# A Strassen form for the FFN input product of a float32 decoder trunk

## The chip, the cores and the metric

The kernel runs on one core of one Trainium2 chip. The metric is the time of one execution on the device in microseconds (us). The core's engines are TensorE (PE in the profile; its weight loads are listed apart as PEld), VectorE (DVE), ScalarE (ACT), GpSimd (POOL) and SyncE (SP), which here only issues loads. Matrix products are written to PSUM, eight banks of 128 x 512 float32; everything else lies in SBUF.

## The reference

A decoder trunk of two layers on 512 tokens of 1024 features. Each layer is: h += 0.5 * FFN(norm(h)), a token mixer (retention in layer 0, forgetting attention in layer 1), h += 0.5 * FFN(norm(h)) with other weights, and a gated input per layer. A last norm follows. The FFN, which runs four times:

```python
def swiglu(x, w_in, w_out):          # w_in 1024 x 5632, w_out 2816 x 1024
    g, u = jnp.split(x @ w_in, 2, axis=-1)
    return (jax.nn.silu(g) * u) @ w_out

def rmsnorm(x, w):
    y = xf * lax.rsqrt(jnp.mean(xf * xf, axis=-1, keepdims=True) + EPS)
    return y * w
```

## The kernel before

Activations lie with features on the partitions: `h` is eight tiles of 128 features x 512 tokens. A float32 operand is kept as two float32r parts, a rounded high one and the remainder as the low one. A product is three matmuls, high x high, high x low and low x high (`mm3`, lines 199 to 202); a high part is a copy on ScalarE and a low part a subtraction, usually on VectorE.

Weights come as chunks of 128 x 1024 in the order of use (`W.plan`). `take` returns the next one and emits the load, copy and subtraction of the chunks up to LOOKAHEAD = 3 further on (lines 79 to 83 and 42 to 55). SP's queue does the loads into three raw tiles; the split parts have four pairs of tiles. In the mixers and in the gated stages the subtraction goes to POOL (`W.low`). The last KEPT chunks stay in SBUF for the final stage, which handles the tokens in two parts of 256.

`Norm.block(b)` makes the operand of the next product from a finished block of h: the gain goes into the split (`halves`), and the squares are summed by ScalarE and POOL (`square`). The token's scale is put on after the product (`rows`).

One FFN (`ffn`, lines 292 to 330) goes over 22 blocks of 128 features. For each the gate and the up chunk are multiplied (`proj`, 8 blocks of input features x 3 matmuls each, 512 columns), then `finish` makes silu(g r) * u and splits it. The output product runs over the 8 blocks of h, each with 22 inner blocks x 3 matmuls in one PSUM bank, evacuated once (lines 326 to 330). The kernel's first two chunks are loaded in narrow parts (`emit_parts`), so that the first products follow x as it comes.

The order of instructions on TensorE is that of the program; on the other engines a planner orders them by program order and its own estimate of what is ready. A tile is written again only after its last reader.

Of the kernel before, what the change touches and what calls it, by code (L numbers as in the profile page):

```python
# [27 lines left out]
LOOKAHEAD = 3  # L28
KEPT = 6


class Weights:
    """Streams weight chunks [128, <=1024] in the order in which they are used, each split
    exactly into two float32r parts, high and low."""

    def __init__(self, nc, raw_pool, split_pool):
        self.nc, self.raw_pool, self.split_pool = nc, raw_pool, split_pool
        self.plan, self.ready, self.used = [], [], 0
        self.low = nc.vector
        self.limit = None  # L40

    def emit(self, upto):
        nc = self.nc
        while len(self.ready) < min(upto, self.limit):
            src = self.plan[len(self.ready)]
            n = src.shape[1]
            raw = self.raw_pool.tile([P, 1024], F32, name="wraw")
            hi = self.split_pool.tile([P, 1024], F32R, name="whi")
            lo = self.split_pool.tile([P, 1024], F32R, name="wlo")
            nc.sync.dma_start(out=raw[:, :n], in_=src)  # L50
            nc.scalar.copy(hi[:, :n], raw[:, :n])  # L51
            self.low.tensor_tensor(  # L52
                out=lo[:, :n], in0=raw[:, :n], in1=hi[:, :n].bitcast(F32), op=ALU.subtract
            )
            self.ready.append((hi, lo))

    def emit_parts(self, count, parts):
        """The first chunks, in narrow parts and side by side."""
        nc = self.nc
        tiles = [  # L60
            (
                self.raw_pool.tile([P, 1024], F32, name="wraw"),
                self.split_pool.tile([P, 1024], F32R, name="whi"),
                self.split_pool.tile([P, 1024], F32R, name="wlo"),
            )
            for _ in range(count)
        ]
        for k0, k1 in parts:
            cs = slice(k0 * P, k1 * P)
            for src, (raw, hi, lo) in zip(self.plan, tiles):  # L70
                nc.sync.dma_start(out=raw[:, cs], in_=src[:, cs])
                nc.vector.tensor_copy(hi[:, cs], raw[:, cs])
                nc.vector.tensor_tensor(  # L73
                    out=lo[:, cs], in0=raw[:, cs], in1=hi[:, cs].bitcast(F32), op=ALU.subtract
                )
            yield
        self.ready += [(hi, lo) for _, hi, lo in tiles]

    def take(self, src):
        assert self.plan[self.used] is src  # L80
        self.emit(self.used + 1 + LOOKAHEAD)
        self.used += 1
        return self.ready[self.used - 1]


@with_exitstack
def trunk(ctx, tc, a):
# [5 lines left out]
    hnpool = ctx.enter_context(tc.tile_pool(name="hnpool", bufs=KB))  # L93
    wraw = ctx.enter_context(tc.tile_pool(name="wraw", bufs=3))
    wsplit = ctx.enter_context(tc.tile_pool(name="wsplit", bufs=LOOKAHEAD + 1))
# [5 lines left out]
    W = Weights(nc, wraw, wsplit)  # L101

# [1 line left out]
    ffn_src = []  # L104
    for i in range(4):
        ins = [(a["ffn_w_in"][i, m], a["ffn_w_in"][i, NF + m]) for m in range(NF)]
        outs = [
            [a["ffn_w_out"][i, m][:, k0 * P : k1 * P] for k0, k1 in ((0, 8), (8, 16), (16, 22))]
            for m in range(KB)
        ]  # L110
        ffn_src.append((ins, outs))
# [10 lines left out]
    def plan_ffn(i):  # L122
        for g, u in ffn_src[i][0]:
            W.plan += [g, u]
        for cs in ffn_src[i][1]:
            W.plan += cs

# [33 lines left out]
    nw = lambda n: small[:, n * 8 : n * 8 + 8]  # noqa: E731  # L161
# [4 lines left out]
    load_x = lambda lo, hi: nc.sync.dma_start(out=hall[:, lo:hi, :], in_=xv[:, lo:hi, :])  # noqa: E731  # L166
# [15 lines left out]
    # the array reaches its full clock while the first loads are under way  # L182
# [5 lines left out]
    def split(src, hi, lo, scale=None):  # L188
        """src * scale = hi + lo."""
# [19 lines left out]
    def over_features(hi, lo):  # L209
        """The sum over the partitions, on all of them."""  # L210
# [6 lines left out]
    class Norm:  # L217
        def __init__(self, gain):
            self.gain, self.hi, self.lo, self.acc = gain, [], [], None

        def halves(self, b):
            hi = hnpool.tile([P, S], F32R, name="hnhi")
            lo = hnpool.tile([P, S], F32R, name="hnlo")
            split(h[b], hi, lo, self.gain[:, b : b + 1])
            self.hi.append(hi)
            self.lo.append(lo)

        def square(self, b, ts_=slice(0, S), keep=False):
            """acc += h[b]^2; or the square is kept by itself."""
# [18 lines left out]
        def rows(self):  # L248
            """[128, 512]: the scale of each token, on all partitions."""
# [6 lines left out]
        def columns(self):  # L256
            """[128, 4]: the scale of token j*128+p on partition p."""
# [12 lines left out]
    def rsqrt(out, v, t):  # L270
        """out = 1 / sqrt(v), with a Newton step; t is scratch."""
# [9 lines left out]
    def proj(srcs, n, out=None, cols=slice(0, S), take=W.take):  # L281
        """[128 features, 512 tokens] of the normed input times each chunk of weights, side by side."""
# [9 lines left out]
    def ffn(i, n, nxt, meanwhile=None):  # L292
        ins, outs = ffn_src[i]
        with tc.tile_pool(name=f"ffn{i}", bufs=NF, reuse_waits="tile") as pool:
            ahi, alo = [], []

            def finish(g, u):
                sg = temp()
                nc.vector.tensor_tensor(out=sg, in0=g, in1=n.r, op=ALU.mult)  # L299
                nc.scalar.activation(sg, sg, AF.Silu)  # L300
                nc.vector.tensor_tensor(out=sg, in0=u, in1=sg, op=ALU.mult)  # L301
                hi = pool.tile([P, S], F32R, name="ahi")
                lo = pool.tile([P, S], F32R, name="alo")
                split(sg, hi, lo)
                ahi.append(hi)
                alo.append(lo)

            first = proj(ins[0], n) + [proj([s], n)[0] for s in ins[1]]
            n.rows()
            finish(*first[0:2])  # L310
            finish(*first[2:4])
            if meanwhile:
                meanwhile()
            for gs, us in ins[2:]:
                finish(proj([gs], n)[0], proj([us], n)[0])
            for m, cs in enumerate(outs):
                o = bank()
                k = 0
                for c in cs:
                    wh, wl = W.take(c)  # L320
                    for j in range(c.shape[1] // P):
                        js = slice(j * P, (j + 1) * P)
                        mm3(o, wh[:, js], wl[:, js], ahi[k], alo[k], k == 0, k == NF - 1)
                        k += 1
# [504 lines left out]
    for _ in first:  # L829
        pass  # L830
# [110 lines left out]
```

## Time and profile before

| | |
|---|---|
| median of 3 runs | 2294.77 us (2294.37 to 2295.56) |
| span of the profiled execution, first to last instruction | 2294.8 us |
| mean granted clock of TensorE | 0.983 |
| HBM read and written | 208.71 MB, 2.13 MB (92 GB/s over the span) |
| first real matmul | at 5.58 us |
| first FFN, windows 16 to 256 and 256 to 376 us | TensorE busy 239.09 and 120.00 us |
| retention, 376 to 781 us | TensorE busy 404.88 us |
| second FFN, 781 to 1140; first gated stage, to 1195 | 359.00 and 55.00 us |
| third FFN, 1195 to 1555; attention, to 1855 | 360.00 and 291.07 us |
| fourth FFN, 1855 to 2216; last stage, to 2295 | 361.00 and 63.99 us |

The profile is of one execution. The runs' times are the spans of the device, so the profiled execution's span can be set against the median directly: they agree to 0.03 us. A row of a group has the instruction's line, engine and operation, output <- inputs, shape and count, then busy time in us and mean duration in ns, then the idle time before it and what ended it. Rows of successive instructions on an engine can overlap.

### The profile page before, as it was taken

How to read it: one execution, taken by the hardware profiler on the slowest of the kernel's cores; microseconds unless marked ns; L12 is line 12 of the kernel's file. 1: busy time of each engine (PE TensorE's matmuls, PEld its weight loads, DVE VectorE, ACT ScalarE, POOL GpSimd, SP SyncE). 2: the span in 40 equal slices, each digit the busy share in tenths (PEclk: the TensorE clock that was granted, in tenths of full speed). 3: DMA queues.
4: the chain of work that ended last, by engine and by line, in shares of the span. 5: the costliest groups of instructions: out<-in, count | busy, mean ns of one | idle time of the engine just before them, and what ended most of it. 6: DMA issues, size and time to landing. Idle time of an engine off the chain costs nothing.

```text
span 2294.8 us, 25481 instructions
## 1 busy us (share of the span) xinstructions
PE 2264.6 (99%) x10157; PEld 1858.3 (81%) x10157; DVE 1108.0 (48%) x1669; ACT 811.7 (35%) x1158; POOL 390.3 (17%) x224
## 2 busy tenths in 40 slices
PE   8999999999999999999999999999999999999998
PEld 6888888888888888888888888887777788888877
DVE  7344332565353654333365444336776664443354
ACT  4223222433333433222243323224565443322233
POOL 1000012444444200000150000003223210000134
PEclk9999999999999999999999999999889999999999
DMA  4333333232222233323323333333222123333331
GB/s 157 101 93 101 92 94 108 88 95 80 89 83 82 93 107 95 101 88 93 100 89 102 99 97 94 92 94 102 74 65 79 60 92 102 101 95 92 93 107 38
DMA packets 63911, 212.49 MB, mean 93 GB/s; under 512 B 7072, under 2 KB 9632, under 8 KB 63792
## 3 DMA queue, kind: packets, MB, share of 16 engines
q1 hardware_dynamic: 62560, 209.78, 29.6%
q8 instruction: 79, 1.29, 0.2%
q10 hardware_dynamic: 1232, 1.09, 0.1%
q14 instruction: 40, 0.33, 0.0%
HBM read 208.71 MB, written 2.13 MB: 92 GB/s over the span
## 4 chain that ended last, share of the span: by engine, by line
PE 95%; DVE 3%; ACT 1%; DMA 0%; issue 0%; SPq 0%; DVEq 0%; ACTq 0%; POOLq 0%
PE bank L200 29%; PE bank L201 29%; PE bank L202 29%; PE bank L357 2%; PE bank L359 2%; PE bank L358 2%; PE bank L608 1%; PE bank L605 1%; DVE q L589 0%; PE bank L655 0%; DVE tlo L192 0%; PE bank L669 0%; PE bank L668 0%; DMA hall<-in_xT 0%; DVE tmp L488 0%
## 5 line engine op out<-in xcount | busy, mean ns | idle before, releaser
L51 ACT CAST whi<-wraw 128x1024 fp32r<-128x1024 f32 (+1 forms) x387 | 399.1, 1034 | 1194.7 <-PE bank L201 683.5
L200 PE MATMUL bank<-hnhi,whi 128*128 128x512 f32 (+1 forms) x1992 | 770.2, 387 | 3.1 <-DVE tmp L750 2.0
L202 PE MATMUL bank<-hnhi,wlo 128*128 128x512 f32 (+1 forms) x1992 | 767.7, 385 | 3.3 <-DVE wlo L73 3.3
L201 PE MATMUL bank<-hnlo,whi 128*128 128x512 f32 (+1 forms) x1992 | 768.0, 386 | 0.4 <-DVE hnlo L195 0.3
L52 DVE TENSOR_TENSOR wlo<-wraw,whi 128x1024 fp32r<-128x1024 f32 (+1 forms) x285 | 341.1, 1198 | 301.6 <-ACT whi L51 285.8
L200 PEld LDWEIGHTS bank<-hnhi,whi 128*128 128x128 f32 x1992 | 379.1, 190 | 78.3 <-DVE tmp L750 2.2
L202 PEld LDWEIGHTS bank<-hnhi,wlo 128*128 128x128 f32 x1992 | 378.2, 190 | 78.8 <-DVE wlo L73 4.5
L201 PEld LDWEIGHTS bank<-hnlo,whi 128*128 128x128 f32 x1992 | 378.8, 190 | 74.8 <-DVE hnlo L195 1.3
L240 POOL TENSOR_TENSOR acc<-acc,tmp 128x512 f32<-128x512 f32 (+1 forms) x68 | 94.2, 1385 | 1445.5 <-ACT tmp L236 1445.0
L52 POOL TENSOR_TENSOR wlo<-wraw,whi 128x1024 fp32r<-128x1024 f32 x102 | 250.6, 2460 | 369.1 <-ACT whi L51 359.6
L200 PE MATMUL bank<-ahi,whi 128*128 128x512 f32 x704 | 277.4, 394 | 0.0
L201 PE MATMUL bank<-alo,whi 128*128 128x512 f32 x704 | 277.4, 394 | 0.0
L202 PE MATMUL bank<-ahi,wlo 128*128 128x512 f32 x704 | 277.4, 394 | 0.0
L301 DVE TENSOR_TENSOR tmp<-bank,tmp 128x512 f32<-128x512 f32 x88 | 60.1, 690 | 257.9 <-PE bank L202 257.9
L200 PEld LDWEIGHTS bank<-ahi,whi 128*128 128x128 f32 x704 | 131.7, 187 | 32.7
L202 PEld LDWEIGHTS bank<-ahi,wlo 128*128 128x128 f32 x704 | 131.6, 187 | 32.6
L201 PEld LDWEIGHTS bank<-alo,whi 128*128 128x128 f32 x704 | 131.7, 187 | 32.5
L299 DVE TENSOR_TENSOR tmp<-bank,rows 128x512 f32<-128x512 f32 x88 | 60.1, 690 | 196.4 <-PE bank L202 196.2
L357 PE MATMUL bank<-whi,hnhi 128*128 128x512 f32 x192 | 74.9, 390 | 0.0
L359 PE MATMUL bank<-whi,hnlo 128*128 128x512 f32 x192 | 74.8, 389 | 0.0
L358 PE MATMUL bank<-wlo,hnhi 128*128 128x512 f32 x192 | 74.7, 389 | 0.0
L326 DVE SCALAR_TENSOR_TENSOR tmp<-bank,rows 128x512 f32<-128x512 f32 x32 | 22.1, 692 | 81.0 <-PE bank L202 81.0
(189 smaller groups left out, 2063.8 us busy)
## 6 DMA issues: line engine op xcount, KB each, us to landing
wraw<-in_ffn_w_in SPq DMA_DIRECT2D x174, 512.0 KB, 3.5
wraw<-in_ffn_w_out SPq DMA_DIRECT2D x64, 512.0 KB, 3.5
wraw<-in_ffn_w_out SPq DMA_DIRECT2D x32, 384.0 KB, 3.1
wraw<-in_ret_qk SPq DMA_DIRECT2D x16, 512.0 KB, 3.6
wraw<-in_ret_v SPq DMA_DIRECT2D x16, 512.0 KB, 3.6
wraw<-in_ret_g SPq DMA_DIRECT2D x16, 512.0 KB, 3.6
wraw<-in_ret_o SPq DMA_DIRECT2D x16, 512.0 KB, 3.5
wraw<-in_ple_gate SPq DMA_DIRECT2D x16, 512.0 KB, 3.6
```

The costliest lines, as they stand in the source:

```text
L51: nc.scalar.copy(hi[:, :n], raw[:, :n])
L52: self.low.tensor_tensor(out=lo[:, :n], in0=raw[:, :n], in1=hi[:, :n].bitcast(F32), op=ALU.subtract)
L200: nc.tensor.matmul(out, wh, xh, start=first, stop=False)
L201: nc.tensor.matmul(out, wh, xl, start=False, stop=False)
L202: nc.tensor.matmul(out, wl, xh, start=False, stop=last)
L240: nc.gpsimd.tensor_tensor(out=self.acc[:, ts_], in0=self.acc[:, ts_], in1=sq, op=ALU.add)
L299: nc.vector.tensor_tensor(out=sg, in0=g, in1=n.r, op=ALU.mult)
L301: nc.vector.tensor_tensor(out=sg, in0=u, in1=sg, op=ALU.mult)
L357: nc.tensor.matmul(os[t], xh, wh[:, js], start=k == 0, stop=False)
L358: nc.tensor.matmul(os[t], xh, wl[:, js], start=False, stop=False)
L359: nc.tensor.matmul(os[t], xl, wh[:, js], start=False, stop=k == KB - 1)
L605: nc.tensor.matmul(at[i], q[e][own[e], i * P : w], klo[own[e], :w], start=True, stop=False)
```

## The change

The input product of a block (its gate and its up features) becomes a 2 x 2 product of halves: the weights by gate or up and by even or odd blocks of input features (A11, A12, A21, A22, each 128 x 512), the input by even or odd blocks and by first or second 256 tokens. In Winograd's form of Strassen's scheme seven products do for eight. Each is 4 blocks x 3 matmuls of 256 columns (`product`). It needs four sums of weights (s1 to s4) and four sums of the input (t1 to t4), with signs so arranged that the output comes out negative, hence -0.5 at the end.

```diff
+LOOKAHEAD = 2
+KEPT = 7
+CHUNKS = ((0, 8), (8, 16), (16, 22))
...
+    def negated(self, raw, hi, lo, src):
...
+        self.nc.scalar.copy(hi, raw)
+        self.nc.scalar.mul(lo, raw, -1.0)
+        self.nc.gpsimd.dma_start(out=lo, in_=src, accum_op=ALU.add)
...
+    def first(self, pair):
...
+        pair.raw = self.load(pair.q)
+        pair.t = self.pool.tile([P, 2, 1024], F32R, name="w8")
+        self.negated(pair.raw, pair.t[:, 0, :], pair.t[:, 1, :], pair.q)
...
+    def emit_sums(self):
...
+        for pair in pairs[: self.pairs_used + 2]:
...
+            add(s1, a21, a22)
+            add(s2, s1, a11)
+            add(s3, a21, a11)
+            add(s4, s2, a12)
+            self.split(su, u[:, 0, :], u[:, 1, :])
+            self.split(s3, w[:, 0, 0:512], w[:, 1, 0:512])
+            self.split(s4, w[:, 0, 512:1024], w[:, 1, 512:1024])
+            self.negated(a12, pair.x[:, 0, :], pair.x[:, 1, :], pair.r[:, 0:512])
```

`pair.q` holds A11 and A22, `pair.r` A12 and A21. The low parts of A11, A22 and A12 are made by a DMA: the negated rounded copy is written, and the raw weights are added to it from HBM by an accumulating load on POOL's queue. `W.low`, so POOL in the gated stages, does the low parts of the sums. `take_pair` asks for the sums of two pairs more than are used.

The input's forms are made by `quarters` in place of `halves`, for the four norms that feed an FFN, with the pair of blocks (2j, 2j+1) as unit: for the even block e a scaled copy, B11 and t1 = e(first) - e(second), for the odd block t2, t3, t4 and the splits of both halves.

```diff
+        def one(m):
+            pair, g, u = live[m]
+            product(g[:, c0], pair.t, 0, n.forms, "b11", True)
+            product(g[:, c1], pair.s12, 0, n.forms, "t1")
+        def two(m):
...
+            product(u[:, c1], pair.s12, 512, n.forms, "t2", True)
...
+            nc.scalar.copy(cc, g)
+            nc.vector.tensor_tensor(out=u[:, c1], in0=u[:, c1], in1=cc[:, c0], op=ALU.add)
...
+            nc.scalar.copy(u2, u[:, c1])
+            nc.vector.tensor_tensor(out=g[:, c1], in0=g[:, c1], in1=u2, op=ALU.add)
...
+        def three(m):
...
+            product(u[:, c0], pair.t, 512, n.forms, "t4")
+            product(g[:, c1], pair.s34, 512, n.forms, "b22")
+            product(u[:, c1], pair.s34, 0, n.forms, "t3")
+            product(g[:, c0], pair.x, 0, n.forms, "b21")
...
+            nc.scalar.copy(u3, u[:, c1])
+            nc.vector.tensor_tensor(out=u[:, c1], in0=u[:, c1], in1=cc[:, c1], op=ALU.add)
+            nc.vector.tensor_tensor(out=u[:, c0], in0=u[:, c0], in1=u3, op=ALU.add)
...
+            for m in range(max(k0, 1), k1):
+                if begun < k1:
+                    start(begun)
+                    one(begun)
+                    two(begun)
+                    begun += 1
+                three(m)
...
+            for ms in ((0, 1), (2,), (3,), (4,), (5,), (6,), (7,)):
+                out_blocks(c, ms)
```

So `three(m)`, which goes on in PSUM banks that VectorE has corrected, follows `one` and `two` of the next block; an FFN begins with `one(0)`, `one(1)`, `two(0)`, `two(1)`, `rows`, `three(0)`. After 8, 16 and 22 blocks the output product of those inner features runs over all of h, and h is updated each time (`out_blocks`); the forms of the next norm are made in the last of the three.

SBUF is re-ordered: operands of 128 x 512 come from four pools of equal tiles (`ua`, `ub`, `uc`, `ud`), an attention tile of values becomes two with two splits each, and the chunks' high and low parts share one tile of a pool of three (`wpool`). Weight sums have two tiles of each kind (`s12`, `s34`, `a12`). The narrow first loads (`emit_parts`) are gone: the first pair is loaded whole, between parts of x, and `Norm.block` follows for each block. `open_ffn` is called ahead of the mixer's last output product and ahead of the gated stage, so that the sums of an FFN's first pairs are made there.

More of the change, by code (lines that the diff above doesn't have):

```diff
@@ L57, in emit_parts @@
-    def emit_parts(self, count, parts):
-        nc = self.nc
[L60 to L77, printed above, removed]
+            self.ready.append(self.first(src) if isinstance(src, Pair) else self.chunk(src))
@@ L289, in proj @@
         return os
-    def ffn(i, n, nxt, meanwhile=None):
-        ins, outs = ffn_src[i]
[L294 to L324, printed above, removed]
```

307 lines of the change are left out of this document (228 added, 79 removed).

## The prediction

> **What bounds the kernel now.** I read the engine table and the chain of waits first.
>
> ```profile
> PE 2264.6 (99%) x10157; PEld 1858.3 (81%) x10157; DVE 1108.0 (48%) x1669; ACT 811.7 (35%) x1158; POOL 390.3 (17%) x224
> PE 95%; DVE 3%; ACT 1%; DMA 0%; issue 0%; SPq 0%; DVEq 0%; ACTq 0%; POOLq 0%
> ```
>
> TensorE (PE) is busy nearly all the time and is 95% of the chain that ended last; VectorE (DVE) is idle half of the span. But matmul rows overlap, so busy time is not a price. The windows view gives one: a stretch that is one whole FFN (the second), a piece of the first FFN's input product, and the last stage, where matmuls are 256 columns wide. Its columns are window, then us busy (instructions) for PE, PEld, DVE, ACT and POOL, then clock, DMA share and GB/s.
>
> ```profile
> 781.00:1140.00 359.00, 359.00 (x1570) 294.02 (x1569) 144.90 (x164) 105.50 (x131) 10.99 (x7) 1.00 0.32 97
> 100.00:200.00 100.00, 100.00 (x443) 82.81 (x442) 39.91 (x45) 28.65 (x36) 0.00 (x0) 1.00 0.32 98
> 2242.00:2262.00 20.00, 20.00 (x171) 20.00 (x170) 9.75 (x24) 9.14 (x20) 13.76 (x17) 1.00 0.00 1
> ```
>
> An FFN issues 22 x 48 + 8 x 66 = 1584 matmuls of 512 columns, so one costs 359/1584 = 0.2266 us; a block of gate and up features (48 of them) costs 10.88 us. The FFNs run without a gap at full clock: only fewer or cheaper matmuls can shorten them. For 256 columns the timeline has the start times (first and last of 25 in an unbroken row):
>
> ```profile
> 2241.44 0.28 PE L200 MATMUL bank<-hnhi,whi 128*128 128x256 f32 x1
> ...
> 2244.27 0.29 PE L200 MATMUL bank<-phi,whi 128*128 128x256 f32 x1
> ```
>
> 24 steps in 2.83 us: 0.118 us each. That is not half of 0.2266 but 52%, and the weight loads (PEld) fill that window, 20.00 of 20.00, against 83% in the window of wide matmuls.
>
> **The change part by part: TensorE.** For one block, seven products of 4 x 3 matmuls with 256 columns replace 48 with 512: 84 x 0.118 = 9.91 us for 10.88. Over 88 blocks that is 88 x 0.97 = **-85 us**, not the eighth of 957 us (120 us) that the columns alone promise. The output product keeps its 528 matmuls per FFN; its three parts add 16 evacuations, each two VectorE operations of 0.69 us (lines 326 and 329, quoted below), beside a part's 5.4 us of matmuls in a stage where VectorE has less to do than in any other: nothing, and without that cover 4 x 16 x 1.4 = 90 us.
>
> The Trainium skill, "TensorE: Matmul & The Clock Gate", section "Back-to-back issue gap", gives N/2.4 + 2.5 ns, 109 ns for 256 columns, and says itself that at small N the weight loads add to it; by it the block would be 9.2 us and the saving, estimated from that page, 150 us. The row here (118 ns) disagrees, so it decides.
>
> **VectorE and ScalarE.** The weights of a block are now summed before they are split, and its products corrected in PSUM. I price one block from these groups (mean ns after the comma):
>
> ```profile
> L52 DVE TENSOR_TENSOR wlo<-wraw,whi 128x1024 fp32r<-128x1024 f32 x253 | 310.4, 1228 | 185.1 <-ACT whi L51 169.3 <-PE bank L212 5.3
> L301 DVE TENSOR_TENSOR tmp<-bank,tmp 128x512 f32<-128x512 f32 x88 | 60.1, 690 | 257.9 <-PE bank L202 257.9
> L192 DVE TENSOR_TENSOR alo<-tmp,ahi 128x512 fp32r<-128x512 f32 x88 | 59.9, 684 | 0.0
> L329 DVE TENSOR_TENSOR hall<-hall,tmp 128x512 f32<-128x512 f32 x32 | 22.1, 692 | 1.1
> L754 DVE TENSOR_TENSOR tmp<-bank,tmp 128x256 f32<-128x256 f32 x16 | 6.8, 424 | 11.5 <-ACT tmp L751 9.0 <-issue 1.9 <-PE bank L789 0.5
> L51 ACT CAST whi<-wraw 128x1024 fp32r<-128x1024 f32 x355 | 372.5, 1052 | 1051.8 <-PE bank L201 540.6 <-issue 457.1 <-PE bank L359 23.9
> L191 ACT CAST ahi<-tmp 128x512 fp32r<-128x512 f32 x88 | 54.5, 621 | 0.5 <-DVE tmp L301 0.5
> L191 ACT CAST thi<-bank 128x512 fp32r<-128x512 f32 x32 | 17.3, 590 | 0.3
> L191 ACT CAST thi<-bank 128x256 fp32r<-128x256 f32 x16 | 6.2, 390 | 0.0
> ```
>
> VectorE: four sums of weights (4 x 0.69), the low half of s1 and s2 together (1.23), of s3 and of s4 (2 x 0.68), four corrections of 256 columns in PSUM (4 x 0.42), two gating products (2 x 0.69), one low half (0.68): **9.1 us**, against 2 x 1.23 + 2 x 0.69 + 0.68 = 4.5 now. ScalarE: three copies of 1024 (3.16), four of 512 (2.48), copies out of PSUM (0.59 + 2 x 0.39), Silu, taken like a cast, and one cast (2 x 0.62): **8.3 us**. Both stand below 9.91, VectorE with 8% left by these durations. More is left by the start times, since rows overlap:
>
> ```profile
> 754.95 0.68 DVE L342 TENSOR_TENSOR hall<-bank,hall 128x512 f32<-128x512 f32 x1
> 755.54 0.74 DVE L484 SCALAR_TENSOR_TENSOR tmp<-bank,small,rn 128x512 f32<-128x512 f32 x1
> ```
>
> 0.59 us from one to the next: about 8 us per block. What TensorE waits for is written early: corrections are due a whole block later (between `two(m)` and the second product of `three(m)` lie `one` and `two` of the next block and one product, 48 matmuls, 5.7 us at least), weights two blocks ahead, and a PSUM bank of eight is reused after four blocks. TensorE runs in written order, so a late correction would hold all the matmuls behind it; but these terms are early by half a block or more. So I cost this work at **nothing** inside the input product; without that cover the period is VectorE's, the second rival.
>
> **The added loads.** Low halves of three of the seven weight blocks (768 KB per block) come from an accumulating DMA on POOL's queue, which waits there for ScalarE's two passes; behind it stand only other such loads (the squares come at a stage's end, and there POOL's sums would wait with it). No row shows one. Its plain neighbour:
>
> ```profile
> wraw<-in_ffn_w_in SPq DMA_DIRECT2D x174, 512.0 KB, 3.5
> ```
>
> From below it is 3.5 us like this; from above I can only say where it decides. A tile of `wpool` comes free about 5.6 us after `start(k)` (36 + 12 matmuls); two ScalarE passes take 2.1 more; it is due two blocks after `start(k)`, at 19.8: 12 us are left. I take twice the plain one, 7 us, and cost it at nothing. The Trainium skill, "Collectives: The Full Stack", section "The bandwidth ceiling: the fold count and why AG ≠ RS ≠ AR", says an add in the DMA path reads two sources and so halves the rate, which is this factor of two; no run yet shows it.
>
> **The starts of the FFNs** give some back. The rows are one matmul's start, line 326's own view (durations, then first and last start), ScalarE's first and last scaled copies of x, two windows (the end of retention, the first gated stage) and POOL's group of low halves:
>
> ```profile
> 5.58 0.63 PE L200 MATMUL bank<-hnhi,whi 128*128 128x512 f32 x1
> L326 DVE SCALAR_TENSOR_TENSOR tmp<-bank,rows x32: 690/691/693, 270.8 to 2217.1; 128x512 f32<-128x512 f32 x32
> 3.78 0.72 ACT L194 ACTIVATE hnhi<-hall,small 128x512 fp32r<-128x512 f32 x1 [1.12 <-DMA small<-in_small]
> 13.65 1.33 ACT L194 ACTIVATE hnhi<-hall,small 128x512 fp32r<-128x512 f32 x2 [0.15 <-DMA hall<-in_xT]
> 759.00:783.00 24.00, 24.00 (x104) 19.40 (x105) 17.47 (x22) 13.79 (x21) 10.84 (x7) 1.00 0.30 92
> 1140.00:1195.00 55.00, 55.00 (x242) 45.06 (x241) 33.47 (x36) 25.19 (x33) 27.05 (x14) 1.00 0.28 91
> L52 POOL TENSOR_TENSOR wlo<-wraw,whi 128x1024 fp32r<-128x1024 f32 x102 | 250.6, 2460 | 369.1 <-ACT whi L51 359.6 <-PE bank L212 6.1 <-issue 3.3
> ```
>
> The first output block is evacuated at 270.8; less its 66 matmuls (15.0) and the input product (239.4) the start now costs 16 us, thanks to narrow first parts of the weights and products that follow the blocks of x one by one. After, every product needs all four pairs of blocks. ScalarE needs for a pair's forms two scaled copies (1.33), three of 256 columns (1.17) and two of 512 (1.24), 1.2 for its squares, and 5.6 for each weight pair (the first two terms above): 4 x 5.0 + 5.6 from 3.8 is 29 us until the last form, 35 with the second pair's weights. By then only `one(0)` (2.8) is done: 32 against 16. As rows overlap, I take **+14** (bounds 0 and 25).
>
> Second and fourth FFN: the forms are made while the mixer's last output product runs, 96 matmuls, 21.8 us. Into that window VectorE gets 8 additions (5.5), four pairs of forms (4 x 4.3: seven operations of 256 columns and two of 512), two chunks (2.5) and the sums of two weight pairs (10.7): 36 us, where the window of 24 us now holds 17.5. At the starting rate above it is 31; TensorE has `one(0)` and `one(1)` (5.7 us) partly to go on with. **+6 each** (bounds 0 and 14). Third FFN: the gated stage lasts 55 us and VectorE has 21 us free against about 16 to add (four pairs of forms for eight plain low halves, the sums), and the sums' low halves go to POOL, at 2.46 us per 1024 columns some 10 us beside the 27 it has: **+4** (0 to 8). TensorE's clock after these idle times, and other small ends: **+3**.
>
> **Sum**: 2294.8 (the span; the median 2294.77 is the same) - 85 + 14 + 12 + 4 + 3 = **2243 us**. With starts at their bounds 2210 to 2274. LOOKAHEAD 2 costs nothing: two chunks of 5.4 us cover 3.5 + 1.1 + 1.2 us. The attention's eight splits cut in two (8 more operations on each of two engines, some 0.4 us) lie beside matmuls.
>
> **The rivals.**
>
> 1. **The accumulating loads set the period** (slower). The window 100 to 200 moved 98 GB/s at a share of 0.32, so about 306 GB/s is full. A block needs 1.05 MB plain and 0.79 MB accumulated at c times the cost: 6.0 us for c = 1, 8.6 for c = 2, 11.1 for c = 3. It decides from c = 2.8, where the period reaches 10.5 and the saving is what the starts cost. At c = 3: 2294.8 + 88 x 0.25 + 33 = **2350**. Against it: the plain loads leave two thirds of the DMA time free. Nothing in the trace excludes it.
>
> 2. **VectorE becomes the bound.** Beside POOL's work its operations with two SBUF inputs stretch:
>
> ```profile
> L488 DVE TENSOR_TENSOR tmp<-tmp,sg 128x512 f32<-128x512 f32 x16 | 18.5, 1176 | 0.0
> ```
>
> 1.18 us for 0.69. If a third of the eight such operations of a block stretch by 0.49, 9.1 becomes 10.4: 2294.8 - 88 x 0.48 + 33 = **2285**. Against it: POOL only issues two loads there. The Trainium skill, "SBUF — State Buffer", section "Who interferes with whom", has two-input VectorE work collide only with POOL instructions that read SBUF; by that nothing stretches, and the forecast stands.
>
> 3. **The starts are hidden** by an order in which forms go ahead of sums: **2220**.
>
> 4. That it does not do what it says: 256-column matmuls at 0.1295 us (10.88/84) would leave no saving; the rows above, with the same operand types, speak against it, and I give it no chance of its own.
>
> **How the numbers follow.** Forecast 0.56 (its own range 2225 to 2274), rival 1 0.16, rival 2 0.18 (0.13 still faster, 0.03 same, 0.02 slower), rival 3 0.10. Faster by over 0.2% (about what a measurement of this kernel can tell from no change): 0.56 + 0.10 + 0.13 = 0.79. Within: 0.04, with 0.01 of rival 1's. Slower: 0.17. The range 2215 to 2312 covers all but rival 1 and the edges, some 0.18.
>
> **What would show it.** Right: starts of the 256-column matmuls 0.118 us apart in the FFN; 9.9 us per block; VectorE about 80 to 90% busy there; TensorE idle some tens of us in all, at four places. Wrong: TensorE waiting in each block, for low halves that a DMA lands (rival 1) or for VectorE's corrections (rival 2); matmuls over 0.125 us apart without a wait.

## The result, and the profile after

The kernel after takes 2442.68 us (median of 4 runs, 2433.86 to 2444.56) against 2294.57 beside it: a ratio of 1.0642, interval 1.0623 to 1.0661. It is 6.4% slower; the forecast was 2243, faster. The profiled execution was the fastest of the four, 2433.86. First the page of the kernel after, engine table and chain of waits:

```profile
PE 2204.2 (91%) x13325; PEld 1961.0 (81%) x13325; DVE 1586.7 (65%) x2695; ACT 1219.4 (50%) x1954; POOL 554.8 (23%) x406
PE 10%; DMA 3%; DVE 2%; ACT 2%; issue 1%; POOL 0%; DVEq 0%; POOLq 0%; ACTq 0%; SPq 0%
```

TensorE is idle for 228 us (30 before). It was 95% of the chain; now the chain can't be followed far and no engine holds it. Over the whole span no other engine has become the bound either: VectorE, which has most to do of them, is at 65%. That pattern, everybody partly idle, points to latency: engines wait for each other in turn. The view of TensorE's waits (releaser, then us in total, times, longest) says what ends its idle times:

```profile
PE bank L413 <- ACT tmp L445: 77.2, 42, 10.7
PE bank L413 <- DMA w<-in_ffn_w_in: 31.2, 8, 4.8
PE bank L413 <- ACT unit_d L314: 30.7, 4, 18.1
PE bank L413 <- ACT unit_a L314: 22.8, 4, 12.3
PE bank L413 <- ACT unit_b L314: 16.2, 2, 9.0
```

L445 is `u2`, ScalarE's copy out of PSUM in the middle of a block's corrections. The second row is the landing of accumulated low parts, always in the first block after a part of the output product. The three L314 rows are forms of x: the starts of the FFNs. What the DMA does stands in the DMA view (queue: packets, MB, share of 16 engines; then issues with size and median us to landing):

```profile
q1 hardware_dynamic: 61984, 209.78, 27.1%
q0 software_dynamic: 25344, 69.22, 16.8%
...
wraw<-in_ffn_w_in SPq DMA_DIRECT2D x176, 512.0 KB, 4.4
...
w<-in_ffn_w_in POOLq DMA_DIRECT2D x88, 512.0 KB, 5.9
...
a<-in_ffn_w_in POOLq DMA_DIRECT2D x88, 256.0 KB, 5.7
```

Per MB the accumulating queue q0 takes (16.8/69.22)/(27.1/209.78) = 1.88 times the DMA time of plain loads, and a plain load now lands in 4.4 us, 3.5 before. A piece of the first FFN's input product, 60 to 140 us, in the windows view (columns as in the prediction):

```profile
60.00:140.00 80.00, 75.19 (x632) 74.17 (x631) 60.79 (x99) 54.25 (x87) 11.36 (x13) 0.99 0.68 162
```

The mean DMA share is 0.68. TensorE loses 4.8 of 80 us here and more in other stretches. One block of it, from the timeline (start, duration, ..., in brackets the idle time before and who ended it), for VectorE (some rows), ScalarE and TensorE (one row):

```profile
81.73 0.42 DVE L457 TENSOR_TENSOR bank<-bank,tmp 128x256 f32<-128x256 f32 x1
...
85.08 0.69 DVE L118 TENSOR_TENSOR sums<-wraw 128x512 f32<-128x512 f32 x1 [2.00 <-DMA wraw<-in_ffn_w_in]
85.69 0.69 DVE L118 TENSOR_TENSOR tmp<-wraw 128x512 f32<-128x512 f32 x1
86.29 0.68 DVE L462 TENSOR_TENSOR tmp<-bank,tmp 128x512 f32<-128x512 f32 x1
```
```profile
82.81 1.06 ACT L93 CAST w<-wraw 128x1024 fp32r<-128x1024 f32 x1 [1.51 <-PE bank L413]
83.77 0.62 ACT L461 ACTIVATE tmp<-tmp 128x512 f32<-128x512 f32 x1
84.30 1.05 ACT L94 ACTIVATE w<-wraw 128x1024 fp32r<-128x1024 f32 x1
87.01 0.62 ACT L257 CAST unit_d<-tmp 128x512 fp32r<-128x512 f32 x1 [1.66 <-DVE tmp L462]
87.53 1.14 ACT L76 CAST s<-tmp 128x512 fp32r<-128x512 f32 x2
88.57 1.04 ACT L76 CAST s<-sums 128x1024 fp32r<-128x1024 f32 x1
89.52 0.62 ACT L93 CAST a<-wraw 128x512 fp32r<-128x512 f32 x1
90.04 0.63 ACT L94 ACTIVATE a<-wraw 128x512 fp32r<-128x512 f32 x1
90.57 0.56 ACT L442 COPY tmp<-bank 128x512 f32<-128x512 f32 x1
91.64 0.37 ACT L445 COPY tmp<-bank 128x256 f32<-128x256 f32 x1 [0.50 <-DVE bank L443]
```
```profile
92.06 0.51 PE L413 MATMUL bank<-unit_b,w 128*128 128x256 f32 x2 [1.05 <-ACT tmp L445]
```

Read it from below. TensorE waits for L445, that for a correction on VectorE, that for the copy L442, and L442 stands on ScalarE's in-order queue behind all the copies of a later pair's weights (L93, L94, L76): it has no idle time ahead of it, so it was only queued. Ahead of the last four of these ScalarE waited 1.66 us for the gating product L462; that stood on VectorE's queue behind two sums of weights (L118), and the first of these had waited 2.00 us for a raw load. So a late plain load, far from TensorE, is passed on to it through the queues of VectorE and ScalarE.

To compare kernels below I use one length beside the time: **the stretch**, from the first addition to x in the FFN's first output part to the FFN's last one (14 of 22 blocks and nearly all of the output product), and what lies outside it. In the second FFN of the kernel after it is 945.0 to 1208.1, 263.1 us. Against the lengths in run e11, below (972.0 us in all four FFNs), the kernel after loses 82.8 us inside the four stretches.

### The profile page after: what moved, and what is told of

The parts are those of the page before. It is cut to its first block, busy times and chain, and to the rows that moved or that the text cites. A ratio compares the mean times of both kernels' runs of the same rounds, so it can differ in the third digit from the quotient of the medians.

```text
span 2432.1 us, 34252 instructions
## 1 busy us (share of the span) xinstructions
PE 2204.2 (91%) x13325; PEld 1961.0 (81%) x13325; DVE 1586.7 (65%) x2695; ACT 1219.4 (50%) x1954; POOL 554.8 (23%) x406
## 3 DMA queue, kind: packets, MB, share of 16 engines
q1 hardware_dynamic: 61984, 209.78, 27.1%
q0 software_dynamic: 25344, 69.22, 16.8%
## 5 line engine op out<-in xcount | busy, mean ns | idle before, releaser
L76 ACT CAST w<-wraw 128x1024 fp32r<-128x1024 f32 (+1 forms) x211 | 213.5, 1019 | 479.5 <-PE bank L268 322.7
L77 POOL TENSOR_TENSOR w<-wraw,w 128x1024 fp32r<-128x1024 f32 x100 | 244.7, 2451 | 347.8 <-ACT w L76 336.4
L268 PE MATMUL bank<-unit_a,w 128*128 128x512 f32 (+1 forms) x752 | 292.0, 388 | 4.6 <-DVE w L77 2.9
L266 PE MATMUL bank<-unit_a,w 128*128 128x512 f32 (+1 forms) x752 | 292.8, 389 | 1.8 <-ACT w L76 1.8
L267 PE MATMUL bank<-unit_a,w 128*128 128x512 f32 (+1 forms) x752 | 291.5, 388 | 0.2 <-DVE unit_a L258 0.2
L266 PE MATMUL bank<-unit_d,w 128*128 128x512 f32 (+1 forms) x744 | 285.5, 384 | 2.6 <-ACT w L76 1.8
L268 PE MATMUL bank<-unit_d,w 128*128 128x512 f32 (+1 forms) x744 | 283.2, 381 | 2.9 <-DVE w L77 2.9
L267 PE MATMUL bank<-unit_d,w 128*128 128x512 f32 (+1 forms) x744 | 283.7, 381 | 0.7 <-DVE unit_d L261 0.5
L413 PE MATMUL bank<-unit_b,w 128*128 128x256 f32 x792 | 164.8, 299 | 126.2 <-ACT tmp L445 77.2
L413 PE MATMUL bank<-unit_b,s 128*128 128x256 f32 x1056 | 243.3, 286 | 0.0
L413 PE MATMUL bank<-unit_d,s 128*128 128x256 f32 x1188 | 198.5, 284 | 4.8 <-ACT unit_d L307 4.2
L413 PE MATMUL bank<-unit_a,s 128*128 128x256 f32 x1188 | 194.9, 281 | 0.0
L95 POOL DMA_DIRECT2D w<-in_ffn_w_in x88 | 77.2, 877 | 507.0 <-ACT w L94 408.4
L413 PE MATMUL bank<-unit_c,s 128*128 128x256 f32 x792 | 183.8, 287 | 0.0
L413 PEld LDWEIGHTS bank<-unit_b,s 128*128 128x128 f32 x1056 | 182.8, 198 | 0.0
L413 PEld LDWEIGHTS bank<-unit_d,s 128*128 128x128 f32 x1188 | 169.5, 196 | 5.3 <-ACT unit_d L307 4.4
L76 ACT CAST s<-sums 128x1024 fp32r<-128x1024 f32 x88 | 92.2, 1048 | 154.3 <-DVE sums L118 149.4
```

Of the source, the lines that this page charges most:

```text
L76: self.nc.scalar.copy(hi, raw)
L77: self.low.tensor_tensor(out=lo, in0=raw, in1=hi.bitcast(F32), op=ALU.subtract)
L95: self.nc.gpsimd.dma_start(out=lo, in_=src, accum_op=ALU.add)
L266: nc.tensor.matmul(out, wh, xh, start=first, stop=False)
L267: nc.tensor.matmul(out, wh, xl, start=False, stop=False)
L268: nc.tensor.matmul(out, wl, xh, start=False, stop=last)
```

## The experiments

Line numbers shift by a few between kernels. Medians are in us; ratios are against the kernel before on the same chip. The runs were made in several sessions on different chips, where the kernel before had medians from 2292.49 to 2295.21, so a difference between two sessions is uncertain by some 3 us.

**Corrections first (e1).** Weights of later pairs are asked for after a block's corrections and gating, not before:

```diff
-        self.take(pair)
+        self.emit(self.used + 1)
+        self.emit_sums()
+        self.used += 1
...
                 three(m)
+                W.advance()
```

> The changed kernel, but the weights of a later pair are asked for after the block's corrections and its evacuation, not ahead of them (same work, other order of the queues). Theory A (order of the queues: corrections stand behind the preparation of weights that wait for tiles TensorE has yet to free): the 77 us that TensorE waits for the copies of the corrections go nearly all, and 5 to 15 us of slow clock with them: about 2355 us, 2335 to 2380. Theory B (VectorE and ScalarE have too much to do per block) and theory C (the accumulating loads are late): the period of a block stays 11 us, 2420 to 2460.

2404.73, ratio 1.048 (1.0451 to 1.051): 38 us back, between the theories of order and of the others. Inside the stretch nothing was gained (266.5 in the second FFN); the gain lies outside, in the first blocks of the FFNs.

**No accumulating loads (e2)**, with the order of the kernel after:

```diff
-        self.nc.gpsimd.dma_start(out=lo, in_=src, accum_op=ALU.add)
```

> The changed kernel without the accumulating loads (the low parts of A11, A22 and A12 are left as the negated rounded copies, so the input product lacks them). Theory C (these loads set the period): all waits inside the input product go, 2330 to 2370. Theory A: only the 31 us go in which TensorE waits for such a load at the first block of an out stage or after it, 2400 to 2425. Theory B: unchanged but for those 31 us.

2322.96, ratio 1.0127 (1.0103 to 1.0151): 120 us back, more than any theory had. The window 60 to 140, waits and a landing of this run:

```profile
60.00:140.00 80.00, 78.69 (x649) 77.22 (x649) 61.08 (x99) 53.62 (x87) 0.00 (x0) 1.00 0.32 99
```
```profile
PE bank L412 <- ACT tmp L444: 39.4, 11, 11.2
```
```profile
wraw<-in_ffn_w_in SPq DMA_DIRECT2D x176, 512.0 KB, 3.5
```

VectorE and ScalarE do what they did (61 and 54 of 80 us); the DMA share falls from 0.68 to 0.32 (and GpSimd's time for issuing these loads goes), and with it the waits: the copy L444 keeps TensorE 11 times in place of 42. The stretch is 242.4. With loads on time the old order was good enough inside it.

**Forms first (e3).** The sums of an FFN's first pairs are made after the forms of x, not ahead of them:

```diff
-        stack = open_ffn(1)
         out_part(ret_o[RH - 1], y[0], y[1], nxt)
-        return stack
+        return open_ffn(1)
```

and so at the other three starts.

> The changed kernel, but the sums of an FFN's first weight pairs are asked for after the forms of its input (open_ffn behind the mixer's output product and the gated stage, not ahead). If the order at the starts costs the 70 us that TensorE waits for forms: half or more of it goes, 2390 to 2410. If it is the amount of work at the starts: the wait only changes its name from forms to sums, 2430 to 2450.

2451.84, ratio 1.0685 (1.0653 to 1.0718): no gain. The waits changed their names:

```profile
PE bank L413 <- ACT s L76: 34.1, 4, 10.1
```

Four waits for split sums (`s`) stand where a part of the waits for forms stood, as the theory of amount has it.

**The thirds alone (e4)**: the kernel before, with its output product in three parts.

```diff
+            for p, (k0, k1) in enumerate(((0, 8), (8, 16), (16, 22))):
+                for m in range(KB):
+                    o = bank()
+                    wh, wl = W.take(outs[m][p])
```

> The kernel before with only the output product taken in three parts of the inner features (eight feature blocks each, h updated three times; the input product still comes whole before it). As predicted, the 16 more evacuations per FFN are hidden: 2290 to 2300. Rival: each part's first chunk or evacuation is late, 1 to 2 us at twelve places: 2305 to 2320.

2295.72, ratio 1.0005 (0.9991 to 1.002): nothing, as costed.

By which way did the loads cost 120 us? In the next four runs, and in e9, the letters A and B stand for two new theories, which their texts spell out.

**Traffic only (e5).**

```diff
-        self.nc.gpsimd.dma_start(out=lo, in_=src, accum_op=ALU.add)
+        out = self.idle_w if lo.shape[1] == 1024 else self.idle_a
+        self.nc.gpsimd.dma_start(out=out, in_=src, accum_op=ALU.add)
```

> The accumulating loads are issued with the same bytes from the same place, but into two tiles that nothing reads (so the output lacks those low parts, and no instruction waits for a landing). Theory A, the transfers take DMA time and so slow the plain loads on which the sums of weights wait: it stays slow, 2390 to 2445, plain loads land in 4.2 to 4.5 us as after the change. Theory B, TensorE is held by the landing of the low halves themselves: it falls to what leaving the loads out gave, 2320 to 2345. Direct waits of TensorE for landings were only 31 us in the changed kernel, so by A at least 2390.

2615.05, ratio 1.1394 (1.1369 to 1.1419), outside both. VectorE's waits say why:

```profile
DVE tmp L482 <- POOL acc L357: 90.2, 5, 71.0
DVE unit_c L312 <- DMA unit_c<-in_ffn_w_in: 87.9, 3, 72.4
```

The unused 2 KB tile came from the pool `uc`, which forms of x use too, so forms waited for its chain of loads, and GpSimd's sums of squares stood behind it. Besides, the loads into the other unused tile waited for no block and were all issued by 566 us, so the traffic lay elsewhere. The run tells nothing of the question.

**Four raw tiles (e6).**

```diff
-    wraw = ctx.enter_context(tc.tile_pool(name="wraw", bufs=3))
+    wraw = ctx.enter_context(tc.tile_pool(name="wraw", bufs=4))
```

> A fourth tile for raw weights, all else as in the changed kernel. Theory A (plain loads made slow by the accumulating ones, and only three tiles to load into, so that VectorE's sums wait for them: 160 us of such waits): a load may start one tile earlier, so these waits shrink to under 60 us and the time falls to 2370 to 2415. Theory B (landing of low halves): no change, 2430 to 2450.

2378.77, ratio 1.0369 (1.0352 to 1.0386), 64 us back, in the range of theory A. VectorE's waits for raw loads, in the kernel after and in this one:

```profile
DVE sums L118 <- DMA wraw<-in_ffn_w_in: 160.4, 69, 8.4
```
```profile
DVE sums L118 <- DMA wraw<-in_ffn_w_in: 55.8, 51, 8.2
```

**Low halves by GpSimd (e7), and with corrections first (e8).**

```diff
         self.nc.scalar.copy(hi, raw)
-        self.nc.scalar.mul(lo, raw, -1.0)
-        self.nc.gpsimd.dma_start(out=lo, in_=src, accum_op=ALU.add)
+        self.nc.gpsimd.tensor_tensor(out=lo, in0=raw, in1=hi.bitcast(F32), op=ALU.subtract)
```

> The accumulating load and ScalarE's negated copy ahead of it are replaced by a subtraction on GpSimd, raw minus high half; the same result. Theory A and B alike: no accumulating transfer, so as when they were left out, 2320 to 2345, with plain loads back at 3.5 us. Rival, two-input work on GpSimd stretches VectorE's two-input work (0.69 to 1.18 us for 512 columns, as one group of the kernel before showed): VectorE's 8.4 us per block become 10 to 11 and it is the bound, 2400 to 2450.

> As e7_low_by_gpsimd, and the weights of later pairs are prepared after a block's corrections and gating instead of before. If the order costs what TensorE still waited for copies out of PSUM without accumulating loads (39 us): 2280 to 2310, about the kernel before. If VectorE is stretched by GpSimd: 2370 to 2420.

2490.45, ratio 1.0863 (1.0843 to 1.0883), and 2478.17, ratio 1.0804 (1.0788 to 1.082): slower than the kernel after, and beyond the rival's ranges too. The first of VectorE's four sums of weights, in the kernel after and in the first of these:

```profile
L118 DVE TENSOR_TENSOR sums<-wraw 128x512 f32<-128x512 f32 x88 | 62.3, 708 | 160.7 <-DMA wraw<-in_ffn_w_in 160.4 <-issue 0.2
```
```profile
L117 DVE TENSOR_TENSOR sums<-wraw 128x512 f32<-128x512 f32 x88 | 126.5, 1437 | 103.0 <-DMA wraw<-in_ffn_w_in 102.8
```

708 ns become 1437; the other three sums take 773 to 859 in e7. So VectorE is stretched as the rival said, but that it becomes the bound is not shown: it is busy for 63.7 of the 80 us of the window 60 to 140 in e7. What grows is TensorE's wait for the copy out of PSUM (line 444 there), 127.6 us for 77.2, which is lateness again. The Trainium skill, "SBUF — State Buffer", section "Who interferes with whom", says that VectorE's work with two SBUF inputs collides with GpSimd instructions that read SBUF, and that DMA doesn't collide with an engine. Both halves are borne out: 1437 ns beside GpSimd's subtraction, and 708 beside accumulating loads against 701 without them.

**Plain loads in place of accumulating ones (e9)**: same bytes, tiles, queue and waits.

```diff
-        self.nc.gpsimd.dma_start(out=lo, in_=src, accum_op=ALU.add)
+        self.nc.gpsimd.dma_start(out=lo, in_=src)
```

> Each accumulating load becomes a plain one: the same bytes from the same place into the same tile, on the same queue, behind the same pass of ScalarE, and waited for by the same matmuls (the low halves then hold the whole weights). Only the DMA time per byte changes, 1.9 times less by the queue rows. Theory A (DMA time that slows the plain loads): a good part of the 120 us comes back, 2350 to 2400, sums' waits for plain loads fall from 160 us to about 110, plain loads land in 3.8 to 4.1 us. Theory B (that a late transfer into the tile exists at all, its landing and its place behind ScalarE and on GpSimd's queue): 2415 to 2445.

2348.56, ratio 1.0239 (1.0222 to 1.0256): 94 of the 120 us come back through DMA time alone; theory B as the whole cause is out. It is not out as a part: TensorE's direct waits for the landings fall as well, from 31.2 to 9.2 us. The DMA view:

```profile
q1 hardware_dynamic: 61984, 209.78, 26.5%
q0 software_dynamic: 25344, 69.22, 9.0%
...
wraw<-in_ffn_w_in SPq DMA_DIRECT2D x176, 512.0 KB, 3.9
w<-in_ffn_w_in POOLq DMA_DIRECT2D x88, 512.0 KB, 4.5
```

q0 costs now 1.03 times what q1 costs per MB (9.0/69.22 against 26.5/209.78), plain loads land in 3.9, VectorE's waits for them fall to 96.6 us, the low halves land in 4.5 instead of 5.9, and the stretch is 246.5.

**Four raw tiles and corrections first, with (e10) and without accumulating loads (e11).**

> The fourth raw tile of e6_four_raw_tiles and the order of e1_corrections_first together, accumulating loads kept; the same result as the kernel after. If the two cure different waits (loads late; copies out of PSUM behind the next weights), the rest of the waits for copies (34 us) goes: 2335 to 2360. If they cure the same wait: 2365 to 2385.

> As e10_four_raw_corrections_first, but the accumulating loads are left out (the output lacks those low parts). What is left then of the change are seven products, the work on VectorE and ScalarE and the starts. If only the loads and the order turned the gain into a loss: 2275 to 2295, at or under the kernel before. If there is a further cost inside the input product: above 2310.

2341.07, ratio 1.0208 (1.0191 to 1.0226), and 2280.27, ratio 0.9947 (0.9934 to 0.9959). The two cures act on different waits, and their gains add: the order gives 38 us without the fourth tile (e1) and 38 with it (e6 to e10), the tile 64 with either order (e6, and e1 to e10). Without accumulating loads the rest of the change is 12 us under the kernel before. With them 61 us remain; 32 of these are the direct waits of TensorE for landings, at the same eight places as in the kernel after.

**Low halves by VectorE (e12)**, in that arrangement: in `negated` `nc.vector.tensor_tensor` in place of the multiplication and the load.

> As e10_four_raw_corrections_first, with the low halves made by VectorE (raw minus high half), without accumulating loads and without ScalarE's negated copies; the same result. VectorE was busy 61.1 of 80 us in a stretch of 8.2 blocks without accumulating loads, 7.4 us per block; 1.23 + 0.68 more is 9.3 against 9.7 of matmuls. If that fits: 2280 to 2315. If VectorE is then the bound or its results come late: 2340 to 2390.

2318.04, ratio 1.0107 (1.0093 to 1.0122), a little over "fits". The window 100 to 200 of this run and of e11:

```profile
100.00:200.00 100.00, 98.82 (x669) 90.59 (x668) 77.23 (x119) 43.17 (x66) 0.00 (x0) 1.00 0.31 101
```
```profile
100.00:200.00 100.00, 98.82 (x669) 90.58 (x668) 66.11 (x104) 51.02 (x77) 0.00 (x0) 1.00 0.30 101
```

The same 669 matmuls: inside the stretch it does fit (242.3). The 38 us that it lost to e11 are outside, 7 to 11 us at each FFN: work on VectorE costs time at the starts.

**What sets the starts** was still open. First the order: the sums of one pair, not of two, ahead of the forms.

```diff
-        for pair in pairs[: self.pairs_used + 2]:
+        for pair in pairs[: self.pairs_used + self.ahead]:
```

`ahead` is 1 until the FFN's first `take_pair`, then 2. In e14 the low halves of the first pair's sums go to GpSimd besides; e15 leaves the low parts out, as e11 does.

> As e12_low_by_vector, but at the start of an FFN only the first pair's weights are summed ahead of the forms of x, the second pair's after them. Theory order: VectorE's queue puts the last two additions to x (done on TensorE at 775.7 in the second FFN of e11_four_raw_corrections_first_no_accumulate, added at 790.6) behind 10.7 us of sums; half of them taken away gives about 5 us at each of three starts, 2298 to 2306. Theory amount: whatever is put back is waited for a little later, 2314 to 2322.

> As e13_one_pair_ahead_low_by_vector, and the low halves of the first pair's four sums are made by GpSimd (2.6 us of VectorE's work at each start, some 5 us of GpSimd's). If VectorE's amount at the start sets it: 6 to 10 us under e13_one_pair_ahead_low_by_vector. If GpSimd beside VectorE stretches the sums as in e7_low_by_gpsimd: the same or up to 10 us over it.

> As e11_four_raw_corrections_first_no_accumulate (low parts left out), with one pair ahead at the starts. Theory order: 2262 to 2270. Theory amount: 2276 to 2284.

2310.12 (ratio 1.0066, 1.0051 to 1.008), 2305.92 (1.0045, 1.0029 to 1.0061) and 2275.70 (0.9919, 0.9906 to 0.9932): the order gave back 8 us from e12 to e13 (9 by the ratios), between the two theories, and 5 from e11 to e15 (6 by the ratios), at the edge of the theory of amount; GpSimd gave 4 more, less than forecast. Order is a small part. Then work was taken away: low halves back to accumulating loads for a third of the bytes (e16, on e14), or for the first two pairs of an FFN only (e17 on e13, e18 on e14).

```diff
+        if [p for p in self.plan if isinstance(p, Pair) and p.ffn == pair.ffn].index(pair) < 2:
+            self.nc.scalar.mul(lo, raw, -1.0)
+            self.nc.gpsimd.dma_start(out=lo, in_=src, accum_op=ALU.add)
+        else:
+            self.nc.vector.tensor_tensor(out=lo, in0=raw, in1=hi.bitcast(F32), op=ALU.subtract)
```

> As e14_one_pair_ahead_low_by_gpsimd_at_start, but in every block the low half of the 256 KB part (a12) comes by the accumulating load again (a third of the accumulated bytes) and leaves VectorE 0.68 us less. Theory amount at the starts (1.9 us less of VectorE's work per pair cost e12 against e11 9 us at each FFN): two such parts per start, 3 us each, 2292 to 2298. If a third of the accumulating traffic slows the plain loads in the steady part: 2310 to 2330.

> As e13_one_pair_ahead_low_by_vector, but in the first two pairs of each FFN, and only there, the low halves come by accumulating loads (3.8 us less of VectorE's work at each start; afterwards VectorE makes them). Theory amount: the 9 us per FFN that e12 lost to e11 come back, 2275 to 2285, under the kernel before. If the landing or the traffic of these few loads holds the start instead: 2305 to 2320.

> As e17_accumulate_first_two_pairs, and the low halves of the first pair's sums made by GpSimd as in e14_one_pair_ahead_low_by_gpsimd_at_start: by amount 4 us under e17, 2270 to 2281; if the accumulating loads then stand on GpSimd's queue behind its subtractions and land late: 2285 to 2310.

2295.87 (1.001, 0.9999 to 1.0021), 2293.23 (0.9997, 0.9988 to 1.0007), 2298.76 (1.0024, 1.0015 to 1.0033). e16 is as forecast by amount. e17 gave back 17 us (16 by the ratios), not 25 to 35, and has the lowest median of the versions that compute the whole result, though e16 can't be told from it: neither differs measurably from the kernel before. In e18 GpSimd's help, worth 4 us in e14, cost 5.5; why stays open.

## Why the prediction was wrong

The account, with each step's forecast beside it. The 91 and the 79 come from e11's stretch: 242.4 us hold 480 matmuls of the output product (108.8 at 0.2266) and 14 x 84 - 36 = 1140 narrow ones, so 133.6/1140 = 0.117 us each, 9.84 per block in place of 10.88.

| step | forecast | found |
|---|---|---|
| narrow matmuls, 88 blocks | -85 | -91 |
| output product in three parts | 0 | 0 (e4) |
| starts (14 + 6 + 4 + 6) and clock (3) | +33 | +79 (e11: -12 = -91 + 79) |
| corrections and weights on time | 0 | +43 (e2 to e11) |
| accumulating loads | 0 | +120 (e2) |
| sum | -52 | +151 |

The found terms sum to 151; measured between the medians, 148. This agreement proves nothing: the steps were taken from the kernel after to e2 to e11, so their differences must add up, and the 3 us are differences between chips. Taken in another order the same steps have other prices: the order of the queues 38, the fourth raw tile 64, and then the accumulating loads 61 (e10 to e11). The tile is worth 64 beside accumulating loads and some 5 without them (43 less 38).

**Right: the matmuls.** The pace was forecast at 0.118 us and is 0.117. (The prediction's 150 us, estimated by the formula of the Trainium skill, "TensorE: Matmul & The Clock Gate", section "Back-to-back issue gap", sets that formula for the narrow matmuls against the measured 0.2266 us of the wide ones; an estimate by the formula for both is 88 x (10.36 - 9.17) = 105 us.) **Right: the thirds**, as far as e4 goes: their evacuations cost nothing. Where one part ends and the blocks go on, the change does lose time, as the next paragraph shows. **Right: VectorE is no bound inside the input product** (rival 2): its sums take 0.71 us there, not 1.18. That rival's mechanism is real, as e7 shows. Inside the input product the change has no computing on GpSimd to set it off; at the starts it has (below).

**Wrong: "12 us are left ... cost it at nothing".** The numbers for the transfer were fair: the factor was taken as 2 (1.88 found), the landing as 7 us (5.9 found). The Trainium skill, "Collectives: The Full Stack", section "The bandwidth ceiling: the fold count and why AG ≠ RS ≠ AR", has an add read two sources and so halve the rate of a collective; the 1.88 here is near that, and no run shows the second read itself. What failed is the conclusion, in two ways.

First, the 12 us hold only where block follows block. In the first block after an output part the low halves do come late: eight waits, 31.2 us in the kernel after and 32.0 in e10. This is the first of them in e10 (GpSimd's issue, then TensorE):

```profile
166.07 0.88 POOL L95 DMA_DIRECT2D w<-in_ffn_w_in  x1 [9.96 <-ACT w L94]
```
```profile
174.07 0.79 PE L419 MATMUL bank<-unit_b,w 128*128 128x256 f32 x2 [4.00 <-DMA w<-in_ffn_w_in]
174.67 0.63 PE L419 MATMUL bank<-unit_a,w 128*128 128x256 f32 x2
175.09 0.63 PE L419 MATMUL bank<-unit_b,s 128*128 128x256 f32 x2
```

ScalarE's copy waited until 163.77 for the output part's matmuls to free the tile; TensorE was ready at 170.07 and got the low halves at 174.07. The matmuls behind the wait start 0.21 us apart, not 0.117 (granted clock 0.74 from 174 to 180), so each wait costs about 6 us: the four stretches of e10 last 1021.3 us, 49 more than the 972.0 of e11.

Second, the other loads became slower, 4.4 us for 3.5, and these feed a loop without slack: three raw tiles, two loads per block, VectorE's sums, ScalarE's copies. In rival 1 I asked only whether the DMA engines fill up as a rate (from c = 2.8). Their mean share was 0.68, but it comes in bursts, as two windows of the kernel after show (in such windows of the kernel before, from 60 to 140, the share is 0.23 to 0.39):

```profile
100.00:105.00 5.00, 4.60 (x40) 4.40 (x39) 4.19 (x9) 3.26 (x7) 0.87 (x1) 1.00 1.03 297
105.00:110.00 5.00, 5.00 (x46) 5.00 (x45) 2.78 (x5) 2.31 (x4) 0.87 (x1) 1.00 0.35 48
```

e6 takes only the shortage of tiles away and gives 64 us back; with four tiles the only long waits left inside the stretches are the eight landings. e9 takes only DMA time away and gives 94 back, by both ways. So rival 1 had the right culprit with the wrong condition: not a rate, but latencies, that of the other loads and that of its own. Its price at c = 3, 2350, counted only the period of a block and was too low.

**Wrong: corrections "early by half a block or more".** I counted the matmuls between `two(m)` and its user, 5.7 us, and not what stands ahead of the copy on ScalarE's queue: the copies for a later pair, which wait in turn for loads and free tiles. The order alone gives 38 us (e1, and e6 to e10), order and fourth tile without accumulating loads 43 (e2 to e11). Nearly all of that lies outside the stretches, in the first blocks of the FFNs. Inside them the order gave nothing in any pair: the four stretches last 1054.8 us in the kernel after and 1064.7 in e1, 1022.3 in e6 and 1021.3 in e10, 975.1 in e2 and 972.0 in e11. The waits for the copy that do stand inside, 24.7 of the 77.2 us, are gone in e6, so they came from late loads.

**Wrong in size: the starts.** FFN ends (last addition to x) are 380.1, 1143.9, 1562.3 and 2218.6 before and 377.3, 1133.0, 1552.0 and 2205.5 in e11. Step by step e11 gains 2.8, 8.1, -0.6 and 2.8; with 22.9 saved in each FFN the starts cost 20, 15, 23 and 20 where 14, 6, 4 and 6 were forecast. The mechanism was near the one forecast, the amount of work on the engines that make sums and forms. Two windows at the second start of e11, some of VectorE's rows there and one of GpSimd's show it:

```profile
775.00:785.00 10.00, 2.34 (x10) 1.49 (x9) 10.00 (x17) 8.28 (x15) 3.50 (x3) 0.76 0.28 106
785.00:795.00 10.00, 2.44 (x10) 2.27 (x11) 9.97 (x15) 8.01 (x13) 2.01 (x2) 0.50 0.33 105
```
```profile
776.09 1.75 DVE L117 TENSOR_TENSOR tmp<-wraw 128x512 f32<-128x512 f32 x1
...
782.26 0.68 DVE L117 TENSOR_TENSOR sums<-wraw 128x512 f32<-128x512 f32 x1
...
790.63 1.28 DVE L528 TENSOR_TENSOR hall<-bank,hall 128x512 f32<-128x512 f32 x2
```
```profile
775.97 1.33 POOL L358 TENSOR_TENSOR acc<-acc,tmp 128x512 f32<-128x512 f32 x1 [2.29 <-ACT tmp L354]
```

VectorE is busy for 19.97 of 20 us, TensorE for 4.78. TensorE finished the products for the last two additions to x by 776; VectorE made them at 790.63, behind sums of weights and forms. A part of VectorE's time there is rival 2's stretch, which the prediction looked for in the input product only: the sum at 776.09 takes 1.75 us beside GpSimd's sum of squares, its like at 782.26 takes 0.68. Seven of VectorE's operations from 755 to 800 are stretched so, each beside one of GpSimd's, by some 7 us together. No run takes the squares off GpSimd, so what this costs in time stays open. At the first start VectorE is busy for 19.0 and ScalarE for 17.9 of the 20 us from 14 to 34, where the forecast counted ScalarE alone. At the third, from 1190 to 1210, VectorE is busy for 16.9 of 20 us, so there the amount is not the whole cause. Order alone gave 5 to 9 us back in all (e13, e15), less work 16 to 17 (e17). The forecast had subtracted `one(0)` and `one(1)` as work that TensorE could go on with, but both stop at the last pair's form. And it had spread the third FFN's forms over a stage of 55 us; the longest of all waits for a form, the 18.1 us of `unit_d` in the rows of waits above, is at the end of that stage.

**The range**, 2215 to 2312, left rival 1 out, and the prediction had no case in which two terms costed at nothing were both wrong.

## What to carry to other kernels

A term costed at nothing because "it is due later" needs its whole chain: for each link, what stands ahead of it on its in-order queue, and how many tiles that loop has; and it needs it at every place where the work changes, here behind each output part. An added transfer is to be priced by what it does to the latency of the loads already there, though the mean share of the DMA engines stays below full. A faster product that needs all of its operand at once pays at every start, and there the engine that makes the operand can be the bound, however idle it is on average.

## What the hardware showed beside that

An accumulating load into SBUF costs 1.88 times a plain one's DMA time per byte, and 1.03 times when the accumulation is taken off (e9). A wait of TensorE costs more than itself: after the idle time at e11's second start the granted clock is 0.50 in the window from 785 to 795, quoted above, and after the wait of 4.00 us in e10 the matmuls start 0.21 us apart. The mean clock fell from 0.983 in the kernel before to 0.955 in the kernel after. An addition of two SBUF tiles on VectorE that takes 0.68 us alone took 1.75 beside one on GpSimd.
